# Re-ordered first stage, whole blocks at the first feed-forward's norm, two-part broadcasts, five pairs in token halves for six and three blocks for four

## The chip, the cores and the metric

The kernel runs on one core of one Trainium2 chip. The metric is the device time of one execution in microseconds (us), the median of several runs. One core has a matrix engine (PE, with its weight loads PEld), a vector engine (DVE), a scalar engine (ACT), a third elementwise engine (POOL), and a queue of transfers that is issued from SP. Each engine takes its own instructions strictly in the order in which the program put them.

## The reference

Two blocks follow each other on one sequence of T = 512 tokens with D = 1024 features, all in float32. Cut to what matters here:

```python
# first block
h = rmsnorm(x, norm1_g); z = h @ w_in + b_in
z_glu, z_rx, z_rg, z_ga, z_gb = split(z)
u   = z_glu[:, :D] * sigmoid(z_glu[:, D:])
u   = silu(layernorm(depthwise_conv31(u)))
y_a = u @ conv_w_out + conv_b_out
xb  = conv4(z_rx)                        # 1280 wide
hb  = rg_lru(xb, wa, wx, lambda)         # gates, then a scan over tokens
y_b = (hb * gelu(z_rg)) @ lru_w_out
x   = x + (sigmoid(z_ga) * y_a + sigmoid(z_gb) * y_b) @ w_mix_out
h   = rmsnorm(x, norm2_g)
x   = x + (silu(h @ ffn_w1) * (h @ ffn_w3)) @ ffn_w2
x   = rmsnorm(x, norm_f_g)
# second block; mods = silu(c) @ w_ada + b_ada gives nine vectors sh, sc, gt
h = rmsnorm(x, g_pre) * (1 + sc1) + sh1
x = x + 0.5 * gt1 * rmsnorm(swiglu(h, w_gu1, w_dn1), g_post)
h = rmsnorm(x, g_pre) * (1 + sc2) + sh2
x = x + gt2 * rmsnorm(token_mixer(h), g_post)    # linear attention + forgetting attention
h = rmsnorm(x, g_pre) * (1 + sc3) + sh3
x = x + 0.5 * gt3 * rmsnorm(swiglu(h, w_gu2, w_dn2), g_post)
```

## The kernel before

Features lie on the 128 partitions and tokens in the free dimension, so a 1024-wide activation is eight tiles of 128x512. Every product is made in three passes of a reduced float format (`mm3`, lines 128 to 130): high part of the weight with high part of the activation, the same weight with the low part, then the weight's low part with the high part. So each activation that feeds a product is kept as a pair (`hi`,`lo`; `u2h`,`u2l`; `m1h`,`m1l`; `pfh`,`pfl`; `hbh`,`hbl`), and each 128x1024 piece of weight that a transfer brings (`st`) is split into `whi` by ACT (line 123) and `wlo` by DVE (line 124; in the first stage POOL makes some). One block of eight feature tiles for 512 tokens is 24 matmuls of 128x512; a block in token halves is 24 of 128x256, twice.

The program is a list `steps`. `add(units, fn, own)` appends a step with the weights it wants. While the steps are emitted in that order, a background list `bg` is worked off between them by a credit that each step's matmuls give (`runbg`), `later` appends to it, `NEXT` in it ends the work of one step, and `flush` empties it. `defer(n, fn)` emits `fn` n steps later. Products write to three rotating accumulation buffers `mm`, everything else to five `ax`.

The first stage follows a string of step names. `g`m makes one eighth of the gated convolution input (two blocks, `ga` and `th`) and starts its 31 taps on DVE in `bg` (line 393). `r`j and `a`/`b` make the inputs and the gates of the recurrence, `s` the scans for five tiles in one step (line 547), `q`j the ten gelu blocks (`ge`, line 557), each multiplied with its scanned tile `xb` and split into `hbh`/`hbl` in the same step. Then eight times `yb_step` (blocks `w_in` 44+m and `lru_w_out`), eight `ga_step` blocks, and eight `ya_step` blocks (`conv_w_out`). The layer norm over the convolution's output (`ln_mean`, `ln_var`, `ln_rstd`, `ln_out`) is pushed to `bg` at the first `yb_step`. A norm's statistics are matmuls with one column per 128 tokens (`rstat`, line 187). The rows are turned into a full tile by a diagonal matrix made on DVE (`diag`, line 208) and one float32 matmul with ones (`bcast2`, line 214), which the trace records as two passes.

At each norm between products a `boundary` runs the last blocks of the product, and the first blocks behind the norm, in two token halves, so that the norm of one half lies beside matmuls of the other. `w_mix_out` runs all eight blocks so; `ffn_w2`, `w_dn1` and `w_dn2` run `NF` = 4 whole and four in halves; behind each norm `NH` = 6 pairs of feed-forward blocks (`ffn_pair`, lines 795 on) run in halves. An `ada_step` brings 512 KB of `w_ada` and multiplies it with `crow` on DVE (line 314); the 72 of them are laid between other steps, 1.75 per block in the first feed-forward.

Of the kernel before, what the change touches and what calls it, by code (L numbers as in the profile page):

```python
# [53 lines left out]
def build(tc, I, O, dbg=None):  # L54
# [128 lines left out]
    def rstat(pc, accs, r):  # L183
        nt = (r[1] - r[0]) // P
        for i, acc in enumerate(accs):
            for j in range(nt):
                mm(pc[:, i * nt + j:i * nt + j + 1], acc[:, r[0] + P * j:r[0] + P * (j + 1)], ones1,  # L187
                   start=True, stop=True)
# [196 lines left out]
    def delay(acc, u, d, w, b, first=False):  # L385
# [166 lines left out]
    def rg_step(j):  # L552
        def fn(W):
# [27 lines left out]
    def yb_step(m):  # L581
# [37 lines left out]
    def ln_out(m):  # L619
        V.tensor_tensor(CV[m], CV[m], H["lnr"], ALU.mult)  # L620
        s = act(CV[m], CV[m], AF.Silu, bias=col("conv_ln_b", m), scale=col("conv_ln_g", m))
        if m == 0:
            with tc.issue_after(s.ins):
                act(crow, crow, AF.Silu)
# [1015 lines left out]
```

## Time and profile before

| | |
|---|---|
| median of 3 runs | 2264.69 us (2263.28 to 2266.47) |
| the profiled execution | 2265.5 us |
| its span (first to last instruction) | 2263.8 us |
| mean granted clock of TensorE, share of full | 0.993 |
| PE busy | 2216.3 us, 98% |
| DVE busy | 1398.2 us, 62% |
| ACT busy | 943.5 us, 42% |
| POOL busy | 154.8 us, 7% |

Busy shares are means over stages with different limits. A matmul's recorded duration overlaps the next one's, so what a matmul costs is read from the distance of two starts. In a timeline row the bracket is the idle time of the engine just before it, with the instruction that ended it. The granted clock has two levels, 1.2 and 2.4 GHz; it is given as a share of the higher.

### The profile page before, as it was taken

To read this page: it belongs to the slowest core of one execution; us is meant where nothing else is said; L and a number is where in the kernel's file an instruction comes from. 1 tells how busy PE (TensorE), PEld (TensorE's weight loads), DVE (VectorE), ACT (ScalarE), POOL (GpSimd) and SP (SyncE) were. 2 spreads that over 40 slices of the span, in tenths; PEclk is the share of its full clock that TensorE was granted. 3 is DMA by queue.
4 is the path that set the end of the run, shared out by engine and by line. 5 is a ranking of instruction groups with operands and counts; after the bars stand their busy time and mean duration, and the time that the engine had idled before them with its cause. 6 is when DMAs were issued, how large, how long until landed. Compare 5 with 4: busy or idle time off the path is not lost.

```text
span 2263.8 us, 31021 instructions
## 1 busy us (share of the span) xinstructions
PE 2216.3 (98%) x12170; PEld 1915.6 (85%) x12170; DVE 1398.2 (62%) x2409; ACT 943.5 (42%) x1538; POOL 154.8 (7%) x178
## 2 busy tenths in 40 slices
PE   8899999999999999999999999999999999999997
PEld 6688788899887899988889987888888899988887
DVE  7999984866766448433326768675656558433234
ACT  6566423634322234332224567663434444323232
POOL 3243220000000000000100021100000000000000
PEclk9999999999999999999999999999999999999999
DMA  5343233524877534323233521213121322432342
GB/s 187 112 118 107 81 108 103 178 93 156 300 246 241 166 109 149 131 93 99 89 103 120 172 86 57 73 42 105 66 80 66 130 89 90 140 102 91 96 118 66
DMA packets 82451, 269.28 MB, mean 119 GB/s; under 512 B 10320, under 2 KB 12624, under 8 KB 82304
## 3 DMA queue, kind: packets, MB, share of 16 engines
q1 hardware_dynamic: 80896, 266.31, 36.6%
q8 instruction: 96, 1.57, 0.3%
q0 software_dynamic: 1264, 0.69, 0.1%
q10 hardware_dynamic: 144, 0.29, 0.1%
q14 instruction: 51, 0.42, 0.1%
HBM read 258.80 MB, written 4.19 MB: 116 GB/s over the span
## 4 chain that ended last, share of the span: by engine, by line
PE 86%; DVE 5%; DMA 2%; issue 1%; ACT 1%; DVEq 0%; ACTq 0%; SPq 0%
PE mm L128 26%; PE mm L129 26%; PE mm L130 26%; DMA st<-w_ada 2%; PE ax L1153 1%; PE ax L1155 1%; DVE wlo L124 1%; PE ax L1154 1%; PE ax L1208 1%; PE ax L214 1%; PE ax L1337 1%; PE ax L187 1%; DVE st L314 0%; DVE ax L393 0%; ACT p L1321 0%
## 5 line engine op out<-in xcount | busy, mean ns | idle before, releaser
L123 ACT ACTIVATE whi<-st 128x1024 fp32r<-128x1024 f32 (+4 forms) x424 | 431.1, 1018 | 838.2 <-PE mm L129 532.5
L124 DVE TENSOR_TENSOR wlo<-st,whi 128x1024 fp32r<-128x1024 f32 (+3 forms) x382 | 454.0, 1189 | 405.1 <-ACT whi L123 403.9
L128 PE MATMUL mm<-pfh,whi 128*128 128x512 f32 (+1 forms) x1676 | 568.9, 339 | 0.5 <-ACT sq L241 0.5
L129 PE MATMUL mm<-pfl,whi 128*128 128x512 f32 (+1 forms) x1676 | 565.6, 338 | 0.0
L130 PE MATMUL mm<-pfh,wlo 128*128 128x512 f32 (+1 forms) x1676 | 564.3, 337 | 1.2 <-DVE wlo L124 1.2
L130 PEld LDWEIGHTS mm<-pfh,wlo 128*128 128x128 f32 x1676 | 316.8, 189 | 34.3 <-DVE wlo L124 1.9
L128 PEld LDWEIGHTS mm<-pfh,whi 128*128 128x128 f32 x1676 | 317.2, 189 | 33.2 <-ACT sq L241 1.3
L129 PEld LDWEIGHTS mm<-pfl,whi 128*128 128x128 f32 x1676 | 317.2, 189 | 31.6 <-issue 0.5
L128 PE MATMUL mm<-m1h,whi 128*128 128x256 f32 (+1 forms) x528 | 177.2, 336 | 4.2 <-DVE fs L795 4.2
L128 PE MATMUL mm<-hi,whi 128*128 128x512 f32 x416 | 165.8, 398 | 15.4 <-ACT hi L341 6.4
L128 PE MATMUL mm<-mh,whi 128*128 128x256 f32 (+1 forms) x528 | 177.5, 337 | 2.0 <-ACT mh L765 1.1
L130 PE MATMUL mm<-mh,wlo 128*128 128x256 f32 (+1 forms) x528 | 177.3, 337 | 0.0
L129 PE MATMUL mm<-ml,whi 128*128 128x256 f32 (+1 forms) x528 | 177.1, 336 | 0.0
L129 PE MATMUL mm<-m1l,whi 128*128 128x256 f32 (+1 forms) x528 | 177.0, 335 | 0.0
L130 PE MATMUL mm<-m1h,wlo 128*128 128x256 f32 (+1 forms) x528 | 176.6, 334 | 0.0
L129 PE MATMUL mm<-lo,whi 128*128 128x512 f32 x416 | 165.9, 399 | 1.1 <-DVE lo L342 1.1
L130 PE MATMUL mm<-hi,wlo 128*128 128x512 f32 x416 | 165.5, 398 | 0.4 <-DVE wlo L124 0.4
L393 DVE SCALAR_TENSOR_TENSOR ax<-th,d_hdw,ax 128x500 f32<-128x500 f32 (+25 forms) x232 | 157.5, 731 | 1.1 <-ACT ax L391 0.2
L314 DVE SCALAR_TENSOR_TENSOR st<-st,crow 128x1024 f32<-128x1024 f32 x72 | 88.0, 1224 | 66.5 <-DMA st<-w_ada 66.0
L795 DVE TENSOR_TENSOR fs<-fs,mm 128x512 f32<-128x512 f32 (+1 forms) x84 | 47.9, 571 | 122.4 <-PE mm L130 122.3
L128 PEld LDWEIGHTS mm<-m1h,whi 128*128 128x128 f32 x528 | 100.2, 190 | 15.8 <-DVE fs L795 5.9
L128 PEld LDWEIGHTS mm<-mh,whi 128*128 128x128 f32 x528 | 100.8, 191 | 13.0 <-ACT mh L765 1.5
(359 smaller groups left out, 3432.8 us busy)
## 6 DMA issues: line engine op xcount, KB each, us to landing
st<-w_gu SPq DMA_DIRECT2D x102, 512.0 KB, 3.3
st<-w_ada SPq DMA_DIRECT2D x72, 512.0 KB, 4.5
st<-ffn_w SPq DMA_DIRECT2D x63, 512.0 KB, 4.1
st<-w_in SPq DMA_DIRECT2D x51, 512.0 KB, 3.3
st<-w2fm SPq DMA_DIRECT2D x51, 512.0 KB, 3.3
st<-w_dn SPq DMA_DIRECT2D x38, 448.0 KB, 3.3
st<-w_dn SPq DMA_DIRECT2D x24, 512.0 KB, 3.5
st<-w2v SPq DMA_DIRECT2D x16, 512.0 KB, 3.3
```

The costliest lines, as they stand in the source:

```text
L123: h = act(hi, src, AF.Copy)
L124: (eng or V).tensor_tensor(lo, src, hi, ALU.subtract)
L128: mm(out, whi, xh, start=start, stop=False)
L129: mm(out, whi, xl, start=False, stop=False)
L130: mm(out, wlo, xh, start=False, stop=stop)
L187: mm(pc[:, i * nt + j:i * nt + j + 1], acc[:, r[0] + P * j:r[0] + P * (j + 1)], ones1, start=True, stop=True)
L214: mm(R[:, :nt * P], ones, dg.rearrange("p n t -> p (n t)"), start=True, stop=True)
L314: V.scalar_tensor_tensor(w, w, 1.0, crow, ALU.mult, ALU.mult, accum_out=mods[:, n:n + 1])
L393: V.scalar_tensor_tensor(acc[:, d:], u[:, :T - d], w, acc[:, d:], ALU.mult, ALU.add)
L795: V.tensor_tensor(s, s, rs(st["u"], r), ALU.mult)
L1153: mm(o, h[:, sl], hi[c], start=k == 0, stop=False)
L1154: mm(o, l[:, sl], hi[c], start=False, stop=False)
```

## The change

Six things are edited.

- **First stage.** `g2` comes two steps earlier and the later `g` steps one; the first convolution taps go through `bg`; the scan of each of the five tiles is deferred by one to five steps; the `hbh`/`hbl` split of a gelu block is deferred by two steps. A zero fill moves from DVE to ACT.
- **`w_ada` steps.** Four lie beside `yb_step`, one behind each `ga_step`, six instead of eight beside `ya_step`, four beside `w_mix_out`, and 1.0 instead of 1.75 per block in the first feed-forward.
- **Broadcasts.** `diag` splits the row into a high and a low part (a cast and a subtraction, four wide) and makes two diagonals; `bcast2` multiplies both in the reduced format into one accumulator, in two single passes.
- **`behind_block`.** The matmuls of `rstat` and `bcast2` are placed behind the end of the product block that was last emitted.
- **First feed-forward's norm.** `w_mix_out` and the blocks behind it run whole. Three pairs multiply x times `norm2_g`, not yet normalized, and scale the result with the norm's rows (`ffn_raw`); the normalized tiles are made in `bg` meanwhile.
- **Halves.** `NH` goes from 6 to 5 and `NF` from 4 to 5.

```diff
+    zero = cp.tile([P, 1], F32, name="zero")
+    ones_r = cp.tile([P, P], F32R, name="ones_r")
...
+    block = [None]
     def mm3(out, whi, wlo, xh, xl, start, stop):
...
-        mm(out, wlo, xh, start=False, stop=stop)
+        block[0] = mm(out, wlo, xh, start=False, stop=stop)
+    def behind_block():
+        return tc.issue_after(block[0].ins) if block[0] is not None else nullcontext()
...
     def diag(y, nt):
-        dg = at(n="dg").rearrange("p (n t) -> p n t", t=P)[:, :nt]
-        V.tensor_tensor(dg, ident.unsqueeze(1).to_broadcast([P, nt, P]),
-                        y.unsqueeze(2).to_broadcast([P, nt, P]), ALU.mult)
-        return dg
+        yp = sp.tile([P, 2, 4], F32R, tag="yp", bufs=8, name=nm("yp"))
+        V.tensor_copy(yp[:, 0, :nt], y)
+        V.tensor_tensor(yp[:, 1, :nt], y, yp[:, 0, :nt], ALU.subtract)
...
+        for q in range(2):
+            dg = at(F32R, "dg").rearrange("p (n t) -> p n t", t=P)[:, :nt]
+            V.tensor_tensor(dg, ident.unsqueeze(1).to_broadcast([P, nt, P]),
+                            yp[:, q, :nt].unsqueeze(2).to_broadcast([P, nt, P]), ALU.mult)
     def bcast2(dg, nt):
         R = pax()
-        mm(R[:, :nt * P], ones, dg.rearrange("p n t -> p (n t)"), start=True, stop=True)
+        with behind_block():
+            for q in range(2):
+                mm(R[:, :nt * P], ones_r, dg[q], start=q == 0, stop=q == 1)
...
-            V.memset(acc[:, 0:d], 0.0)
+            act(acc[:, 0:d], zero[:, 0:d], AF.Copy)
...
             for m in range(5):
                 j = g * 5 + m
-                V.tensor_tensor(XB[j], XB[j], GT[2, j], ALU.mult)
-                V.tensor_tensor_scan(XB[j], GT[0, j], XB[j], 0.0, ALU.mult, ALU.add)
+                defer(1 + m, lambda j=j: scan(j))
...
-            HB[j] = (at(F32R, "hbh"), at(F32R, "hbl"))
-            split(ge, *HB[j])
+            def parts():
+                HB[j] = (at(F32R, "hbh"), at(F32R, "hbl"))
+                split(ge, *HB[j])
+            defer(2, parts)
...
-    for it in ("g0 r0 r1 r2 r3 r4 g1 a0 r5 a1 g2 a2 r6 a3 g3 a4 r7 r8 s0 g4 r9 b0 g5 b1 g6 b2 g7 b3 b4 "
+    for it in ("g0 r0 r1 r2 r3 r4 g1 g2 a0 r5 a1 g3 a2 r6 a3 g4 a4 r7 r8 s0 g5 r9 b0 g6 b1 b2 g7 b3 b4 "
...
-        if m >= 8:
+        if m % 2:
             ada_step()
...
     def ln_push(W):
+        bg.extend([NEXT, NEXT])
         later(0.9, ln_mean)
...
         add(wunits("w_in", 36 + m, KT, [8]), fn)
+        ada_step()
...
+    def ffn_raw(u, PF, j):
+        def fg(W):
+            gemm(pg, W, H["xg"])
+            V.tensor_tensor(s, pg, H["R"], ALU.mult)
+            act(s, s, AF.Silu)
+        def fu(W):
+            gemm(pu, W, H["xg"])
+            V.tensor_tensor(t, pu, H["R"], ALU.mult)
+            V.tensor_tensor(t, t, st["s"], ALU.mult)
+            split(t, *PF[j])
+        ada_step()
...
-    NH = 6
-    NF = 4
+    NH = 5
+    NF = 5
...
-    boundary("w_mix_out", M1, [8], mix_done, 0, n2_half, ffn_first(u1, PF1))
+    NR = 3
+    mix_steps()
+    add([], n2_rows)
+    for j in range(NR):
+        ffn_raw(u1, PF1, j)
...
-        H["ada"] = H.get("ada", 0.0) + 1.75
+        H["ada"] = H.get("ada", 0.0) + 1.0
...
-    ffn_rest(u1, PF1, ada_between)
+    for j in range(NR, NFF):
+        ffn_pair(u1, PF1, j, FULL, between=ada_between)
```

How the program's order moves is seen at three places. The first is PE at the layer norm of the convolution (`lnm` is the sum for its mean, `lnv` that for its variance, `hi`/`lo` are read by `ga_step`, `u2h`/`u2l` by `ya_step`). Before:

```order
L130 MATMUL mm_3060<-hi_433,wlo_2923 128x512
L187 MATMUL ax_3088<-ones,lnm_1582 128x1 x4
L128 MATMUL mm_3116<-hi_419,whi_2964 128x512
L129 MATMUL mm_3116<-lo_420,whi_2964 128x512
L130 MATMUL mm_3116<-hi_419,wlo_2965 128x512
L128 MATMUL mm_3116<-hi_421,whi_2964 128x512
L129 MATMUL mm_3116<-lo_422,whi_2964 128x512
L130 MATMUL mm_3116<-hi_421,wlo_2965 128x512
L128 MATMUL mm_3116<-hi_423,whi_2964 128x512
L214 MATMUL ax_3097<-dg_3095,ones 128x512
L129 MATMUL mm_3116<-lo_424,whi_2964 128x512
```

After:

```order
L136 MATMUL mm_3262<-hi_443,wlo_3174 128x512
L198 MATMUL ax_3289<-ones,lnm_1603 128x1 x4
L239 MATMUL ax_3303<-dg_3299,ones_r 128x512
L239 MATMUL ax_3303<-dg_3301,ones_r 128x512
L198 MATMUL ax_3340<-ones,lnv_3306 128x1 x4
L239 MATMUL ax_3367<-dg_3363,ones_r 128x512
L239 MATMUL ax_3367<-dg_3365,ones_r 128x512
L134 MATMUL mm_3424<-u2h_3372,whi_3213 128x512
L134 MATMUL mm_3466<-u2h_3372,whi_3256 128x512
L134 MATMUL mm_3508<-u2h_3372,whi_3418 128x512
L135 MATMUL mm_3424<-u2l_3373,whi_3213 128x512
```

The norm's four groups stood among the `ga_step` blocks; now they stand behind the last of these (`mm_3262`) with no product between them, and the first `ya_step` blocks follow.

The second is ACT at the first gelu blocks (`tt` belongs to the scans of the first five tiles). Before:

```order
L557 ACTIVATE ge_1843<-mm_1818,pcol 128x512
L123 ACTIVATE hbh_1846<-ge_1843 128x512
L123 ACTIVATE whi_1914<-st_1747 128x1024
L557 ACTIVATE ge_1885<-mm_1860,pcol 128x512
L543 ACT_TABLE_LOAD
L543 ACTIVATE tt_1399<-tt_1399 128x512
L123 ACTIVATE hbh_1888<-ge_1885 128x512
```

After:

```order
L595 ACTIVATE ge_1810<-mm_1785,pcol 128x512
L127 ACTIVATE whi_1860<-st_1721 128x1024
L595 ACTIVATE ge_1848<-mm_1823,pcol 128x512
L579 ACT_TABLE_LOAD
L579 ACTIVATE tt_1461<-tt_1461 128x512
L579 ACTIVATE tt_1596<-tt_1596 128x512
L579 ACTIVATE tt_1629<-tt_1629 128x512
L579 ACTIVATE tt_1741<-tt_1741 128x512
L579 ACTIVATE tt_1772<-tt_1772 128x512
L127 ACTIVATE hbh_1866<-ge_1810 128x512
```

The split `hbh` of a gelu block, which needs DVE's product with the scanned tile, stood right behind that block's gelu; now at least one more gelu goes ahead of it.

The third is PE at the boundary behind `w_dn1`, where the normalized first half of `h` is first read by the block of 48 columns. Before:

```order
L129 MATMUL mm_10389<-pfl_7928,whi_10535 128x256
L130 MATMUL mm_10389<-pfh_7927,wlo_10536 128x256
L128 MATMUL mm_10389<-pfh_7992,whi_10535 128x256
L214 MATMUL ax_10533<-dg_10504,ones 128x256
L129 MATMUL mm_10389<-pfl_7993,whi_10535 128x256
L130 MATMUL mm_10389<-pfh_7992,wlo_10536 128x256
```

After:

```order
L136 MATMUL mm_9655<-pfh_7845,wlo_9725 128x256
L239 MATMUL ax_9801<-dg_9772,ones_r 128x256 x2
L134 MATMUL mm_9944<-pfh_7017,whi_9774 48x256
L134 MATMUL mm_10005<-pfh_7017,whi_9804 128x256
L135 MATMUL mm_9944<-pfl_7018,whi_9774 48x256
L136 MATMUL mm_9944<-pfh_7017,wlo_9775 48x256
```

The broadcast was followed by 77 matmuls of the product's other half before the first 48-column one; now that one is next.

Counted over the whole order, product matmuls of 256 columns fall by 1548 and those of 512 rise by 774; broadcasts fall from 7 of 512 and 16 of 256 columns to 8 and 14.

## Rows read from the trace of the kernel before

**Rows 1.** Page, part 1: busy time, share and instructions of each engine.
```profile
PE 2216.3 (98%) x12170; PEld 1915.6 (85%) x12170; DVE 1398.2 (62%) x2409; ACT 943.5 (42%) x1538; POOL 154.8 (7%) x178
```

**Rows 2.** Timeline of PE (start, duration, instruction): six matmuls of a whole block apart.
```profile
999.91 0.39 PE L128 MATMUL mm<-pfh,whi 128*128 128x512 f32 x1
...
1001.27 0.39 PE L128 MATMUL mm<-pfh,whi 128*128 128x512 f32 x1
```

**Rows 3.** Timeline of PE: twelve matmuls of a block in halves apart.
```profile
869.87 0.28 PE L128 MATMUL mm<-pfh,whi 128*128 128x256 f32 x1
...
871.31 0.28 PE L128 MATMUL mm<-pfh,whi 128*128 128x256 f32 x1
```

**Rows 4.** Windows: length, busy PE PEld DVE ACT POOL (instructions), clock, DMA share, GB/s.
```profile
60.00:94.00 34.00, 24.47 (x86) 17.98 (x85) 33.84 (x51) 18.02 (x28) 7.87 (x7) 0.85 0.43 117
...
230.00:246.00 16.00, 12.26 (x43) 9.53 (x42) 16.00 (x20) 5.51 (x8) 3.67 (x2) 0.79 0.24 74
340.00:380.00 40.00, 40.00 (x180) 32.88 (x180) 14.23 (x16) 13.36 (x17) 4.16 (x3) 1.00 0.32 109
600.00:700.00 100.00, 99.30 (x437) 81.56 (x435) 65.62 (x96) 25.74 (x33) 0.00 (x0) 1.00 0.76 249
```

**Rows 5.** Timeline of PE at the first gelu blocks; the second row is 14 matmuls later.
```profile
236.49 0.79 PE L128 MATMUL mm<-hi,whi 128*128 128x512 f32 x1 [3.74 <-ACT ge L557]
...
242.56 0.40 PE L130 MATMUL mm<-hi,wlo 128*128 128x512 f32 x1
```

**Rows 6.** Timeline of PE at the layer norm, to the first `ya_step` block.
```profile
375.42 0.95 PE L187 MATMUL ax<-ones,lnm 128*128 128x1 f32 x8
376.23 0.49 PE L128 MATMUL mm<-hi,whi 128*128 128x512 f32 x1
...
377.71 0.39 PE L128 MATMUL mm<-hi,whi 128*128 128x512 f32 x1
377.95 1.02 PE L214 MATMUL ax<-dg,ones 128*128 128x512 f32 x2
...
379.03 0.40 PE L130 MATMUL mm<-hi,wlo 128*128 128x512 f32 x1
...
406.80 0.39 PE L128 MATMUL mm<-u2h,whi 128*128 128x512 f32 x1
```

**Rows 7.** Timeline of DVE at the end of the layer norm.
```profile
394.44 0.16 DVE L193 SCALAR_TENSOR_TENSOR s<-s,s 128x4 f32<-128x4 f32 x1
394.64 0.69 DVE L208 TENSOR_TENSOR dg<-ident,s 128x512 f32<-128x512 f32 x1
395.83 1.23 DVE L124 TENSOR_TENSOR wlo<-st,whi 128x1024 fp32r<-128x1024 f32 x1 [0.50 <-ACT whi L123]
396.98 4.27 DVE L620 TENSOR_TENSOR cv<-cv,ax 128x512 f32<-128x512 f32 x7
```

**Rows 8.** Timeline of PE: a half-width broadcast; one matmul lies between the rows.
```profile
505.60 0.67 PE L214 MATMUL ax<-dg,ones 128*128 128x256 f32 x2
...
506.23 0.28 PE L130 MATMUL mm<-m1h,wlo 128*128 128x256 f32 x1
```

**Rows 9.** Waits of PE: us in total, times, longest.
```profile
PE mm L128 <- DVE fs L795: 4.8, 5, 1.9
```

**Rows 10.** Timeline of DVE in the first feed-forward.
```profile
720.92 1.23 DVE L314 SCALAR_TENSOR_TENSOR st<-st,crow 128x1024 f32<-128x1024 f32 x1 [2.10 <-DMA st<-w_ada]
```

**Rows 11.** Timeline of PE behind `w_dn1`, then behind `w_out`.
```profile
1236.64 0.70 PE L214 MATMUL ax<-dg,ones 128*128 128x256 f32 x2 [0.23 <-DVE dg L208]
...
1247.13 0.28 PE L128 MATMUL mm<-pfh,whi 128*48 128x256 f32 x1
...
1873.92 0.67 PE L214 MATMUL ax<-dg,ones 128*128 128x256 f32 x2 [0.84 <-DVE dg L208]
1875.71 0.38 PE L128 MATMUL mm<-mh,whi 128*128 128x256 f32 x1 [1.12 <-ACT mh L765]
```

**Rows 12.** Timeline of DVE behind `w_dn1`: the last low parts of the first half.
```profile
1243.97 1.27 DVE L766 SCALAR_TENSOR_TENSOR pfl<-ht,mods,pfh 128x256 fp32r<-128x256 f32 x3
```

More of the change, by code (lines that the diff above doesn't have):

```diff
@@ L102, in build @@
     G.memset(ones, 1.0)
+    zero = cp.tile([P, 1], F32, name="zero")
+    G.memset(zero, 0.0)
+    ones_r = cp.tile([P, P], F32R, name="ones_r")
+    G.memset(ones_r.bitcast(F32), 1.0)
     eps1 = cp.tile([P, 1], F32, name="eps1")
@@ L184, in rstat @@
         nt = (r[1] - r[0]) // P
[L185 to L188, printed above, removed]
+        with behind_block():
+            for i, acc in enumerate(accs):
+                for j in range(nt):
+                    mm(pc[:, i * nt + j:i * nt + j + 1], acc[:, r[0] + P * j:r[0] + P * (j + 1)], ones1,
+                       start=True, stop=True)
     def newton(y, t, a):
@@ L313, in fn @@
             w = W[0][:, 0]
+            if n == 0:
+                with tc.issue_after(EV[0].ins):
+                    act(crow, crow, AF.Silu)
             V.scalar_tensor_tensor(w, w, 1.0, crow, ALU.mult, ALU.mult, accum_out=mods[:, n:n + 1])
@@ L436, in convolve, with first @@
             def convolve():
-                taps(0, 2)()
-                with behind(raw):
-                    taps(2, 4)()
+                if len(bg) > 3:
+                    bg.insert(len(bg) - 3, (0.0, taps(0, 2)))
+                else:
+                    taps(0, 2)()
+                    bg.append(NEXT)
+                def first():
+                    with behind(raw):
+                        taps(2, 4)()
+                later(1.44, first)
                 for d in range(4, 31, 4):
@@ L620, in ln_out @@
         V.tensor_tensor(CV[m], CV[m], H["lnr"], ALU.mult)
[L621 to L624, printed above, removed]
+        act(CV[m], CV[m], AF.Silu, bias=col("conv_ln_b", m), scale=col("conv_ln_g", m))
         U2.append((at(F32R, "u2h"), at(F32R, "u2l")))
@@ L662, in fn @@
             M1.append((hi, lo))
-        add(wunits("conv_w_out", m, KT, [8]), fn, own=1.8)
-        ada_step()
+        add(wunits("conv_w_out", m, KT, [8]), fn, own=2.1)
+        if m < 6:
+            ada_step()
     pool_steps[1] = len(steps)
@@ L735, in acc_sumsq, with mix_g, mix_steps, done @@
         sumsq(H[key], src, r, first, scale=scale)
-    def mix_done(ps, m, r):
-        V.tensor_tensor(rs(X[m], r), rs(X[m], r), ps, ALU.add)
-        acc_sumsq("acc", rs(X[m], r), m, r)
+    def mix_g(m):
+        h, l = H["xg"][m]
+        act(h, X[m], AF.Copy, scale=col("norm2_g", m))
+        V.scalar_tensor_tensor(l, X[m], col("norm2_g", m), h, ALU.mult, ALU.subtract)
+    def mix_steps():
+        def done(ps, m, r):
+            if m == 0:
+                H["xg"] = pairs(KT)
+            V.tensor_tensor(X[m], X[m], ps, ALU.add)
+            mix_g(m)
+            acc_sumsq("acc", X[m], m, FULL)
+        for m in range(KT):
+            product("w_mix_out", M1, [8], done, [m], FULL, 2.9)
+            if 1 < m < 6:
+                ada_step()
+    def n2_rows(W):
+        R = rms_rows(H["acc"], FULL)
+        H["R"] = at(n="R")
+        act(H["R"], R, AF.Copy)
+        del H["acc"]
+    def n2_tiles(m0):
+        def f():
+            if m0 == 0:
+                H["h"] = M1
+            for m in range(m0, m0 + 2):
+                t = at(n="ht")
+                V.scalar_tensor_tensor(t, X[m], col("norm2_g", m), H["R"], ALU.mult, ALU.mult)
+                post_split(m, t, FULL)
+        return f
+    def n2_end(W):
+        flush()
+        del H["xg"], H["R"]
+        SH[0] = lambda m: mods[:, m:m + 1]
+    def ffn_raw(u, PF, j):
+        st = {}
+        ug, uu = u(j)
+        def fg(W):
+            pg = pmm()
+            gemm(pg, W, H["xg"])
+            s = st["s"] = at(n="fs")
+            V.tensor_tensor(s, pg, H["R"], ALU.mult)
+            act(s, s, AF.Silu)
+        def fu(W):
+            pu = pmm()
+            gemm(pu, W, H["xg"])
+            t = at(n="fu")
+            V.tensor_tensor(t, pu, H["R"], ALU.mult)
+            V.tensor_tensor(t, t, st["s"], ALU.mult)
+            PF.append((at(F32R, "pfh"), at(F32R, "pfl")))
+            split(t, *PF[j])
+        add([ug], fg, own=0.7)
+        add([uu], fu, own=2.1)
+        ada_step()
     def normed(r, R, pre):
```

28 lines of the change are left out of this document (15 added, 13 removed).

## Prediction
> **What bounds the kernel now.** I read the page's busy times first: PE is busy for 98% of the span [rows 1], so the time is PE's, and a change can only give back time in which PE idles, runs at the low clock, or does the same product in a dearer form. I then read PE's timeline for what one matmul costs, by the distance of starts. In a whole block six matmuls take 1001.27 - 999.91 = 1.36 us, 0.2267 us each [rows 2]. In halves twelve take 1.44 us, 0.120 each [rows 3], so two halves cost 0.240, that is 13.3 ns more than one whole. Windows come next, for stretches where PE is not fed: in 60 to 94 us PE started 86 matmuls, worth 86 x 0.2267 = 19.5 us of 34, so 14.5 us were lost to waits and to a granted clock whose mean is 0.85; DVE is busy 33.84 of these 34 us. At the first gelu blocks it is the same picture, DVE busy 16.00 of 16 [rows 4]. Elsewhere in the front DVE has room: in 340 to 380 us it is busy 14.23 of 40 [rows 4]. Last I read the layer norm and the boundaries, since the order moves work there.
>
> **The change part by part.** All sums are against the profiled execution, 2265.5 us; the median of the runs is 0.8 lower.
>
> *Halves.* 774 pairs of half matmuls become whole ones: 774 x 13.3 ns = 10.3 us less, all of it on PE [rows 2, 3]. These blocks lie where PE is otherwise fed, so I count it fully.
>
> By the Trainium skill, "TensorE: Matmul & The Clock Gate", section "Back-to-back issue gap", an isolated matmul's gap is its columns over 2.4 GHz plus about 2.5 ns; a pair would then lose 2.5 ns, and 774 pairs 1.9 us, not 10.3. The rows here say 13.3 ns, so the trace does not agree, and the rows decide.
>
> *Broadcasts behind the layer norm.* A 512-wide one costs 379.03 - 377.71 less two matmuls of 0.2267 = 0.87 us [rows 6]; a 256-wide one 506.23 - 505.60 less 0.12 = 0.51, with any wait in it [rows 8]. Before there are 4 and 16 behind the layer norm: 3.5 + 8.2 = 11.7 us. The new form has two single passes. No row of before shows it; if a pass costs what a product matmul costs, 5 and 14 of them are 5 x 0.453 + 14 x 0.24 = 5.6 us, 6 less. Against it DVE makes two four-wide operations of 0.2 us (394.44 to 394.64) and a second diagonal before PE may start [rows 7], which costs where PE already waits for the diagonal, as behind `w_out` [rows 11]. Bounds are -6 and 0; I take -4.3, nearer the passes, since most broadcasts have product matmuls ahead of them.
>
> *Fewer `w_ada` steps in the first feed-forward.* PE waits 4.8 us there for `fs` on DVE [rows 9], and DVE stands before it in front of a `w_ada` tile that has not landed, 2.10 us in the row [rows 10]; traffic is 249 GB/s [rows 4]. A block of 24 matmuls takes 5.44 us and brings 0.5 MB of its own, and 0.875 MB of `w_ada` before, 0.5 after: some 258 GB/s become 193. I take -4.4 of the 4.8; bounds -4.8 and 0.
>
> *`w_dn1` boundary.* Before, the first 48-column block starts 10.5 us after the broadcast that its input needs [rows 11]; the 77 half matmuls between cover the chain. In the new order that block is next. From broadcast to first product took 1.8 us behind `w_out`, where nothing covers it either [rows 11], and the last low part of this half came 1243.97 + 1.27 - 1236.64 = 8.6 us after the broadcast [rows 12], while the first 48 interleaved half matmuls need 5.8. So 1.8 to 2.8 for the tail, plus a later broadcast by the longer diagonal, plus low clock: +4, bounds 0 and +8.
>
> *Un-normalized first blocks, handover, tail.* `w_mix_out` whole puts the end of the last tile, the statistics and the broadcast beside the first pair, which needs only x times a column. What is late next is the eviction of that pair, which waits for the norm's rows, and the eight normalized tiles before the fourth pair. I cost both at +1, bounds -1 and +4; the cover is about 130 us of matmuls, and DVE has a third of its time free in 600 to 700 us [rows 4].
>
> *Front, until the last `ga_step` block.* Its parts are three. The wait at the gelu blocks is 3.74 us, then 14 matmuls take 6.07 us instead of 3.17 at the low clock [rows 5]: 6.6 us. ACT there held a `hbh` split, which waits for DVE behind five scans, in front of the next gelu. With the split two blocks later and the scans spread, I count all 6.6 as gone. The layer norm's two statistics (376.23 - 375.42 = 0.8 each) and two broadcasts (0.87 each) no longer cut into these blocks [rows 6]: 3.3. For the 14.5 us of 60 to 94 the bounds are 0 and all of it: `g2` two steps earlier gives PE two more blocks (10.9 us) to do before `a0`, but DVE is full, and each tap, gate and split still has to be done before its reader. Following the new order through ACT and DVE with the rows' durations I find three waits left there, about 7 us, so -8 rather than -14.5. The last `ga_step` block then ends at 406.8 - 17.9 = 388.9.
>
> *Layer norm.* This is the price. Before, its chain lay beside `ga_step` blocks, and `ya_step` began at 406.80 without a wait [rows 6]. In the new order PE has only the norm's own matmuls between the last `ga_step` and the first `ya_step`, so it idles for the chain. From the first statistics to the first `cv` times the norm's factor took 396.98 - 375.42 = 21.6 us [rows 6, 7]. In it DVE did four weight splits of 1.15 (395.83 to 396.98), now one: -3.4. Two row splits of 0.4 and two more diagonals of 0.6: +2.0. Two single-pass broadcasts: -0.8. Then one `cv` pass of 0.6 and two ACT passes of about that length before the first matmul: +1.9. Sum 21.3, bounds 18 and 25. Behind so long an idle time I expect the low clock: rows 5 price it at 2.9 after a shorter one, and with `u2` tiles arriving one by one I take +3.4, bounds 2.9 and 7. DVE also gets 12 `w_ada` steps of 1.15 us before the norm (13.8 us), and six weight splits (6.9) that stood behind the norm's start. I cost them at nothing, since 25.8 us are free in 340 to 380 [rows 4]; without that cover they delay the norm one for one. `ya_step` starts at 388.9 + 21.3 = 410.2.
>
> *Sum.* Front -8 - 6.6 - 3.3 + 21.3 + 3.4 = +6.8. Behind it -10.3 - 4.3 - 4.4 + 4 + 1 = -14.0. Together -7.2: 2258.3 for a profiled execution, 2257.5 as median.
>
> **The rivals.** *A, the front is freed:* the 60 to 94 us waits go nearly whole and the `w_dn1` chain is covered after all: -6.5 and -3, 2248. For it: two more blocks of cover are worth 10.9 us. Against: DVE is full there [rows 4].
>
> *B, slower:* DVE reaches the end of the convolution's taps late. The norm needs the last tap's sum, PE has nothing else to do, and each us is paid in full. DVE is full until the scans, gets 20.7 us more to do, and PE arrives some 18 us earlier. Against it stand the idle 25.8 us. It decides once `ya_step` starts 12 us later than I say, past 422; at 12 to 20 late the time is 2270 to 2278.
>
> *C, the waits in 60 to 94 only move:* 0 of the 8, 2265.5, no change. For it: DVE's full window. Against: the earlier `g2` is product work that needs little of DVE.
>
> *D, halves cost next to nothing:* the 13.3 ns would belong to those stretches (weights or operands there), not to the width, and whole blocks in the same places would keep most of it; at 2.5 ns a pair the sum loses 8.4: 2266. That is what the skill's gap rule, cited above, would make of it. Against: the two spacings are steady where nothing waits [rows 2, 3].
>
> **How the numbers follow.** Forecast 0.45 (2251 to 2263 by itself), A 0.20, B 0.17, C 0.12, D 0.06. A measurement of this kernel can tell about 0.2% from no change, 4.5 us: faster is below 2260.2, slower above 2269.2. Faster: A and three quarters of the forecast, 0.54. Slower: B, 0.17. Within: the rest, 0.29. For the range I reach down into A and up to B's lower edge, 2244 to 2271; it leaves out A's lower part and most of B.
>
> **What would show it.** In the profile after: one idle stretch of PE of about 20 us at the layer norm, ended by ACT's `u2h`, with a low clock behind it, and `ya_step` near 410; no wait for `ge`; whole blocks still 0.2267 us a matmul; PE's waits for `fs` near zero; a wait of some us right behind `w_dn1`'s first broadcast. The prediction is wrong if PE does something else in that stretch, if the norm starts clearly after the last `ga_step` block, or if 60 to 94 us still loses 14.

## The result, and the profile after

The change made the kernel slower: 2282.13 us median (2280.86 to 2285.66) beside 2264.12 for the kernel before, a ratio of 1.0088 (95% interval 1.0074 to 1.0101). I had forecast 2257.5 within 2244 to 2271. The span of the profiled execution went from 2263.8 to 2279.2 us, 15.4 more.

The page of the kernel after shows that PE did not get more to do. Its busy time fell by 9.1 us against [rows 1]; its idle time rose.

```profile
PE 2207.2 (97%) x11394; PEld 1878.8 (82%) x11394; DVE 1396.3 (61%) x2379; ACT 928.4 (41%) x1494; POOL 159.6 (7%) x180
```

The starts of the same blocks in PE's two timelines tell where the 15.4 us arise:

| PE's first matmul of | before | after | ahead or behind |
|---|---|---|---|
| the gelu blocks | 199.95 | 199.61 | -0.3 |
| `ga_step` | 359.10 | 356.13 | -3.0 |
| `ya_step` | 406.80 | 423.47 | +16.7 |
| `w_mix_out` | 450.46 | 468.54 | +18.1 |
| `ffn_w2` | 747.78 | 753.89 | +6.1 |
| a block late in the attention (`pfh`) | 1592.95 | 1609.78 | +16.8 |
| end of the span | 2263.8 | 2279.2 | +15.4 |

There are two losses, 19.7 us between the start of `ga_step` and that of `ya_step`, and 10.7 between `ffn_w2` and the attention, and one gain, 12.0 us from `w_mix_out` to `ffn_w2`.

The first loss is the bare layer norm. PE's timeline from the last `ga_step` block on (start, duration, instruction, and in brackets idle time and what ended it; only rows with a wait):

```profile
400.42 1.05 PE L198 MATMUL ax<-ones,lnm 128*128 128x1 f32 x8 [0.60 <-POOL lnm L494]
402.73 1.40 PE L239 MATMUL ax<-dg,ones_r 128*128 128x512 f32 x2 [1.26 <-DVE dg L230]
413.94 1.84 PE L198 MATMUL ax<-ones,lnv 128*128 128x1 f32 x8 [9.82 <-DVE lnv L267]
419.31 1.30 PE L239 MATMUL ax<-dg,ones_r 128*128 128x512 f32 x2 [3.53 <-DVE dg L230]
423.47 1.65 PE L134 MATMUL mm<-u2h,whi 128*128 128x512 f32 x3 [2.85 <-ACT u2h L127]
```

The same four groups lay among product matmuls before [rows 6]. From the first statistics to the first `ya_step` matmul it is 23.05 us, and DVE's timeline shows why: the norm is a chain on DVE, one pass behind the other, with nothing in PE's order that it could do meanwhile.

```profile
404.33 2.47 DVE L654 TENSOR_TENSOR cv<-cv,ax 128x512 f32<-128x512 f32 x4
...
411.52 2.28 DVE L267 TENSOR_TENSOR lnv<-lnv,sq 128x512 f32<-128x512 f32 x3
...
418.48 1.29 DVE L230 TENSOR_TENSOR dg<-ident,yp 128x512 fp32r<-128x512 f32 x2
420.65 3.08 DVE L661 TENSOR_TENSOR cv<-cv,ax 128x512 f32<-128x512 f32 x5 [0.89 <-PE ax L239]
```

What DVE did just ahead of the chain matters too. The sum for the mean (`lnm`) needs the last total of the convolution (`cv`, L462), and that stands on DVE behind ten `w_ada` steps that each waited for their tile to land: 22.0 us of such waits between 345 and 400 us, and none there in the kernel before.

```profile
395.96 1.23 DVE L342 SCALAR_TENSOR_TENSOR st<-st,crow 128x1024 f32<-128x1024 f32 x1 [2.50 <-DMA st<-w_ada]
...
398.25 0.68 DVE L462 TENSOR_TENSOR cv<-cv,ax 128x512 f32<-128x512 f32 x1
```

PE came only 0.60 us too early for `lnm` in this run. In the trace of "Four blocks in halves again", whose first stage is the same, PE came 2.8 us earlier than here and the norm began no sooner:

```profile
400.72 1.87 PE L198 MATMUL ax<-ones,lnm 128*128 128x1 f32 x8 [3.71 <-POOL lnm L494]
```

Windows of the kernel after (length; busy us and instructions of PE, PEld, DVE, ACT, POOL; clock; DMA share; GB/s) stand beside [rows 4]:

```profile
60.00:94.00 34.00, 26.55 (x101) 20.69 (x100) 32.45 (x47) 15.06 (x25) 8.09 (x7) 0.90 0.44 124
230.00:246.00 16.00, 16.00 (x72) 13.27 (x71) 15.82 (x19) 6.87 (x11) 4.46 (x2) 1.00 0.14 49
380.00:427.00 47.00, 28.94 (x117) 22.83 (x116) 31.94 (x61) 17.59 (x27) 1.29 (x1) 0.75 0.35 112
600.00:700.00 100.00, 100.00 (x443) 82.81 (x442) 56.45 (x75) 29.20 (x37) 0.00 (x0) 1.00 0.63 197
1200.00:1300.00 100.00, 90.64 (x708) 88.28 (x707) 66.70 (x171) 45.14 (x88) 1.04 (x2) 0.97 0.37 119
```

The wait at the first gelu blocks is gone (72 matmuls instead of 43 in 230 to 246). In the first feed-forward PE does not wait any more and the traffic is 197 GB/s instead of 249. Behind `w_dn1` PE is busy for 90.64 of 100 us. The kernel before, in its own window, was nearly full:

```profile
1200.00:1300.00 100.00, 98.47 (x806) 97.07 (x805) 70.08 (x170) 51.47 (x101) 0.99 (x2) 1.00 0.43 142
```

### The profile page after: what moved, and what is told of

It reads as the page before. It is cut to its first block, busy times and chain, and to the rows that moved or that the text cites. A ratio compares the mean times of both kernels' runs of the same rounds, so it can differ in the third digit from the quotient of the medians.

```text
span 2279.2 us, 29354 instructions
## 1 busy us (share of the span) xinstructions
PE 2207.2 (97%) x11394; PEld 1878.8 (82%) x11394; DVE 1396.3 (61%) x2379; ACT 928.4 (41%) x1494; POOL 159.6 (7%) x180
## 4 chain that ended last, share of the span: by engine, by line
PE 80%; DVE 11%; DMA 2%; issue 2%; ACT 1%; POOL 0%; DVEq 0%; ACTq 0%; POOLq 0%
PE mm L134 24%; PE mm L135 24%; PE mm L136 23%; DVE ax L421 3%; DMA st<-w_ada 2%; DVE wlo L128 1%; PE ax L1246 1%; PE ax L1247 1%; PE ax L1248 1%; PE ax L1301 1%; PE ax L1430 1%; PE ax L198 1%; DVE xb L582 1%; PE ax L239 0%; DVE xb L581 0%
## 5 line engine op out<-in xcount | busy, mean ns | idle before, releaser
L128 DVE TENSOR_TENSOR wlo<-st,whi 128x1024 fp32r<-128x1024 f32 (+4 forms) x365 | 434.2, 1191 | 414.6 <-ACT whi L127 413.8
L134 PE MATMUL mm<-pfh,whi 128*128 128x512 f32 (+2 forms) x1592 | 553.9, 348 | 5.6 <-DVE qb L1128 2.8
L135 PE MATMUL mm<-pfl,whi 128*128 128x512 f32 (+2 forms) x1592 | 552.1, 347 | 0.6 <-DVE pfl L868 0.6
L136 PE MATMUL mm<-pfh,wlo 128*128 128x512 f32 (+2 forms) x1592 | 551.5, 347 | 0.8 <-DVE wlo L128 0.8
L134 PEld LDWEIGHTS mm<-pfh,whi 128*128 128x128 f32 (+1 forms) x1592 | 302.5, 190 | 40.9 <-issue 3.0
L136 PEld LDWEIGHTS mm<-pfh,wlo 128*128 128x128 f32 (+1 forms) x1592 | 302.5, 190 | 36.8 <-DVE wlo L128 1.2
L135 PEld LDWEIGHTS mm<-pfl,whi 128*128 128x128 f32 (+1 forms) x1592 | 302.4, 190 | 35.1 <-DVE pfl L868 1.0
L134 PE MATMUL mm<-mh,whi 128*128 128x512 f32 (+1 forms) x512 | 174.6, 342 | 3.4 <-ACT fs L890 2.0
L136 PE MATMUL mm<-mh,wlo 128*128 128x512 f32 (+1 forms) x512 | 174.2, 341 | 0.0
L135 PE MATMUL mm<-ml,whi 128*128 128x512 f32 (+1 forms) x512 | 173.9, 341 | 0.0
L134 PEld LDWEIGHTS mm<-mh,whi 128*128 128x128 f32 x512 | 97.8, 191 | 14.6 <-ACT fs L890 2.2
```

The source lines that it names most:

```text
L128: (eng or V).tensor_tensor(lo, src, hi, ALU.subtract)
L136: block[0] = mm(out, wlo, xh, start=False, stop=stop)
```

## The experiments

Ratios are against the kernel before on the same chip. "PE's loss" in a stretch is the sum, over its matmuls, of the distance between two starts less what that form takes when nothing waits (0.2267 us for 512, 0.120 for 256 columns). It is 3.6 us for the kernel before and 14.6 for the one after in 1200 to 1300 us.

### The layer norm back among the `ga_step` blocks

```diff
-        bg.extend([NEXT, NEXT])          # ahead of the layer norm
...
-        if m % 2:                        # beside yb_step
-            ada_step()
-        ada_step()                       # behind ga_step
-        H["ada"] = H.get("ada", 0.0) + 1.0
+        H["ada"] = H.get("ada", 0.0) + 1.3
-        runbg((slack - prep) * (1.3 if ln_steps[0] <= i < ln_steps[1] else 1.0))
+        runbg((slack - prep) * (3.0 if ln_steps[0] <= i < ln_steps[1] else 1.0))
```

> Edit on the changed kernel: the twelve w_ada steps beside yb_step and ga_step go into the first feed-forward (1.3 per block instead of 1.0), the two NEXT entries ahead of the layer norm go, and the credit factor in that stage is 3.0 instead of 1.3; in the order the norm's statistics and broadcasts then stand among the ga_step blocks again. Theory (the norm's bare chain costs the time): PE's idle stretch of 23 us before the first ya_step block goes to under 3 us, ya_step starts near 405 us instead of 423.5, and the time falls by 14 to 20 us to 2262 to 2268; the first feed-forward may give 0 to 3 us back to w_ada waits. Rival (DVE is behind with the taps, so the norm cannot start earlier whatever its place): the wait moves to PE's statistics matmul among the ga_step blocks, ya_step still starts after 418, and the time falls by 5 us or less, 2277 or more.

Measured 2271.85 us, ratio 1.0045 (1.0028 to 1.0062). PE's timeline, rows with a wait:

```profile
390.21 0.95 PE L198 MATMUL ax<-ones,lnv 128*128 128x1 f32 x8
406.69 0.80 PE L134 MATMUL mm<-u2h,whi 128*128 128x512 f32 x1 [4.91 <-ACT tha L684]
```

The second statistics now run 16 us ahead of `ya_step`, which starts at 406.69 instead of 423.47. So DVE's taps were not behind. This run changes the norm's place and takes the twelve `w_ada` steps out of DVE's way at once; the last experiment parts the two. Which of the two edits, the `NEXT` entries or the `w_ada` steps, put the norm behind the last `ga_step` block was not tried singly. By the ratios the time fell by 10 to 14 us and not by the 17 at `ya_step`: the twelve `w_ada` steps that had to go into the first feed-forward brought its waits for `fs` back (3.5 us). My lower bound of 14 us was too high. The 4.91 us left before `ya_step` are not the chain alone: the first `u2h` is done by 402.9, but the wait ends with ACT's `tha`, which reads the accumulation buffer of an earlier `ga_step` block and stands on ACT behind the norm's next tiles:

```profile
405.97 0.67 ACT L684 ACTIVATE tha<-mm,d_hb_in 128x512 f32<-128x512 f32 x1
```

### Four blocks in halves again

```diff
-    NF = 5
+    NF = 4
```

> Edit on the changed kernel: NF 4 instead of 5, so four blocks of ffn_w2, w_dn1 and w_dn2 run in halves again. Theory (cover lost at w_dn1): the waits of 1.2, 2.2, 0.6, 1.7, 0.9 and 3.0 us between 1250 and 1297 us and the low clock behind them go mostly, minus 9, against 66 more pairs in each of three places, 3 x 66 x 13.3 ns = 2.6 us: 2275, range 2273 to 2278. Rival (those waits come from the placing behind a block, or from the longer diagonal, not from the number of blocks): they stay, and the time rises by 2.6 us to 2285.

Measured 2281.12 us, ratio 1.0084 (1.0065 to 1.0104), no clear difference to the changed kernel (1.0088, 1.0106). PE's loss in 1200 to 1300 us went from 14.6 to 12.4 only. The wait before the 48-column block went, but one of 2.9 us (for ACT's `sq`) took its place, and the 2.8 for DVE's `qb` stayed. Neither account had this: the cover came back, and the loss did not go.

### Only the old string of steps

```diff
-    "g0 r0 r1 r2 r3 r4 g1 g2 a0 r5 a1 g3 a2 r6 a3 g4 a4 r7 r8 s0 g5 r9 b0 g6 b1 b2 g7 b3 b4 "
+    "g0 r0 r1 r2 r3 r4 g1 a0 r5 a1 g2 a2 r6 a3 g3 a4 r7 r8 s0 g4 r9 b0 g5 b1 g6 b2 g7 b3 b4 "
```

> Edit on the changed kernel: only the string of the first stage's steps is that of before. Theory (with DVE full the waits of the first 200 us only move with the order): the first gelu block starts within 2 us of the 199.6 of both kernels, and the time is 2282 within 3 us. Rival (the order does save the 8 us that I had put on it, and something else in the new first stage takes it back): the first gelu block starts at 205 or later and the time is 2288 or more.

Measured 2283.01 us, ratio 1.0096 (1.0080 to 1.0112), between the two of the changed kernel. The first gelu block did start later, at 205.2 us, behind a wait of 4.18 us for `gt`, as the rival had it; by the first `ga_step` block the two were level (357.6 beside 357.8 in the changed kernel's second trace), and the time is the theory's. The order moves waits within the first stage and takes none out of it as a whole. (The string moves more than the list of the change says: `g2` and `g3` come three steps earlier, `g4` four, `g5` two, `g6` one, and `g7` stays.)

### Float32 broadcasts again

```diff
-        for q in range(2):               # diag: two diagonals of the split row
+        V.tensor_tensor(dg, ident..., y..., ALU.mult)
-                mm(R[:, :nt * P], ones_r, dg[q], start=q == 0, stop=q == 1)
+            mm(R[:, :nt * P], ones, dg, start=True, stop=True)
```

> Edit on the changed kernel: diag and bcast2 in float32 as before (one diagonal, one matmul in two passes), still placed behind the last block. My forecast (PE time of the passes decides): slower by 4 us, 2286. Rival (DVE's longer chain decides, since PE waits 16 us for dg in all after the change and 4.5 us before): faster by 3 to 8 us, 2274 to 2279, with PE's waits for dg down by about 0.6 to 1.0 us each.

Measured 2275.28 us (2272.22 to 2281.69), ratio 1.0064 (1.0041 to 1.0086). That is below the changed kernel's 1.0088 and 1.0106, against my forecast, but the intervals overlap; the runs spread widely here, and the profiled one was the slowest of them. In that trace the stretch from `ffn_w2` to the attention is 4.3 us shorter than in the changed kernel's first trace (851.6 beside 855.9).

### The changed kernel again

> The changed kernel itself, beside the others on the same chip, so that small differences can be read: 2279 to 2283.

Measured 2282.93 us, ratio 1.0106 (1.0083 to 1.0129); with the first run that gives 1.0088 to 1.0106 for the changed kernel, between chips. Its trace has the same waits as its first one.

### The whole first stage as before

All hunks of the diff up to the layer norm are undone, with 1.3 `w_ada` steps per block; broadcasts, placing, whole blocks and halves stay new.

> Edit on the changed kernel: the whole first stage as before (string, taps, scans, splits, zero fill, no w_ada step beside yb_step and ga_step, no NEXT ahead of the norm), with 1.3 w_ada steps per block in the first feed-forward; broadcasts, placing, whole blocks and halves stay new. Theory (the first stage's new order is worth nothing beside the norm, and the later loss sits behind w_dn1): ya_step starts near 407, and the time is that of e1_ln_early within 3 us. Rival (the new order of the first stage does help, and only the norm's place hurt): 5 us or more slower than e1_ln_early.

Measured 2273.54 us, ratio 1.0061 (1.0038 to 1.0084), `ya_step` at 408.43. By the ratios that is 0.16%, 3.6 us, above the first experiment, with overlapping intervals: beside the norm's place no gain of the first stage's new order can be told from noise.

### No placing behind the last block

```diff
     def behind_block():
-        return tc.issue_after(block[0].ins) if block[0] is not None else nullcontext()
+        return nullcontext()
```

> Edit on the changed kernel: behind_block places nothing, so statistics and broadcasts go where the scheduler puts them. Theory (their late place is part of the loss behind w_dn1: the statistics of the second half stand 26 rows earlier in the new order without it): PE's loss between 1200 and 1300 us falls from 14.6 to about 10, elsewhere little changes, 2276 to 2279 beside 2281. Rival (the placing costs nothing, the statistics matmuls cut into blocks instead): within 2 us of the changed kernel. The layer norm's idle stretch of 23 us stays in both.

Measured 2281.49 us, ratio 1.0094 (1.0075 to 1.0112); PE's loss in 1200 to 1300 us 15.3. The placing by itself is not a cause.

### The first feed-forward's part alone

The kernel before with `mix_steps`, `ffn_raw`, and the `w_ada` steps that go with them.

> The kernel before with one part of the change alone: w_mix_out and the first feed-forward whole, three pairs not normalized, and the w_ada steps that belong to it (six beside ya_step, four beside w_mix_out, 1.3 per block). Theory (this part carries the whole gain: 480 pairs x 13.3 ns = 6.4 us and most of 4.8 us of waits for fs, less about 2 for the handover): faster than before by 7 to 11 us, first product of ffn_w2 at 737 to 741 us instead of 747.8. Rival (the gain in that stretch came from the broadcasts or from having w_ada out of the way earlier): faster by 4 us or less.

Measured 2259.82 us, ratio 0.9994 (0.9983 to 1.0005): no difference that can be told, and short of the 7 us forecast. From `w_mix_out` to `ffn_w2` it took 291.2 us instead of 297.3, about the 6.4 us of 480 pairs; the waits for `fs` did not go. Of PE's waits (us in total, times, longest), beside [rows 9]:

```profile
PE mm L134 <- DVE fs L854: 4.9, 5, 1.9
```

In this trace the first stage was 2.7 us later at `ya_step` than in the kernel before, which I can't put down to an edit.

### Early norm, and the boundary as before

The first experiment's edits, with `NF` 4, float32 broadcasts and no placing.

> The changed kernel with the edits of e1_ln_early, and with NF 4, float32 broadcasts and no placing, so that the boundary behind w_dn1 stands as before; the new first stage, the first feed-forward and NH 5 stay. Theory (two causes, the norm's bare chain and the lost cover behind w_dn1, make up the whole loss): PE's loss between 1200 and 1300 us falls from 14.7 to under 5, ya_step starts near 407, and the time is that of the kernel before less 0 to 4 us: 2258 to 2264. Rival (a third cause, such as the new first stage or the w_ada traffic): still 2267 or more.

Measured 2259.48 us, ratio 0.9981 (0.9972 to 0.9990), 0.19% faster than the kernel before and the fastest version found. The window behind `w_dn1` is full again (PE's loss 3.7 us), so the two losses together make up the whole of the result (the run undoes several edits at once and does not part them):

```profile
1200.00:1300.00 100.00, 98.49 (x799) 96.70 (x799) 71.69 (x171) 52.32 (x104) 0.98 (x2) 1.00 0.45 145
```

### The broadcasts alone

The kernel before with the changed `diag` and `bcast2`, nothing else.

> The kernel before with the two-part broadcasts alone. My forecast's step (the passes on PE decide): faster by 4 us, by up to 6. What e4_fp32_bcast points to (DVE's longer chain ahead of the broadcast decides at every boundary): slower by 3 to 7 us, with PE's waits for dg up from 4.5 to about 12 us.

Measured 2271.95 us, ratio 1.0033 (1.0021 to 1.0045): slower by 7.5 us. PE's passes did get cheaper; these are the groups of the two widths (count, busy us, mean ns, idle before), first of the kernel before, then of this one:

```profile
L214 PE MATMUL ax<-dg,ones 128*128 128x256 f32 x32 | 10.8, 431 | 4.9 <-DVE dg L208 4.5
L214 PE MATMUL ax<-dg,ones 128*128 128x512 f32 x14 | 7.4, 612 | 0.2
```

```profile
L229 PE MATMUL ax<-dg,ones_r 128*128 128x256 f32 x32 | 7.9, 330 | 7.4 <-DVE dg L216 7.0
L229 PE MATMUL ax<-dg,ones_r 128*128 128x512 f32 x14 | 5.9, 432 | 0.6 <-DVE dg L221 0.5
```

That is 4.4 us less busy time and 2.9 more idle time in front of them; I had expected those waits for `dg` to grow to about 12 us. Most of the loss is not at the broadcasts at all: PE's loss in 1200 to 1300 us is 7.0 us above that of the kernel before. Its largest parts are two waits a little behind the broadcasts of `w_dn1`, on PE, with low clock behind the first (mean 0.91 in 1240 to 1260 us):

```profile
1240.78 0.39 PE L130 MATMUL mm<-pfh,whi 128*128 128x256 f32 x1 [2.94 <-ACT sq L256]
```

The other, of 2.8 us, stands at 1284.5 and ends with DVE's `qb`. In the kernel before the first one is 0.47 us. ACT's timelines show the difference. `sq<-mm` reads an accumulation buffer that the next block needs. Before, it stands behind two of the norm's high parts:

```profile
1237.89 0.91 ACT L765 ACTIVATE pfh<-ht,mods 128x256 fp32r<-128x256 f32 x2 [2.19 <-DVE ht L946]
1238.71 0.36 ACT L241 ACTIVATE sq<-mm 128x256 f32<-128x256 f32 x1
1238.97 0.90 ACT L765 ACTIVATE pfh<-ht,mods 128x256 fp32r<-128x256 f32 x2
```

With the two-part broadcasts a weight split and four high parts go ahead of it:

```profile
1237.81 1.06 ACT L125 ACTIVATE whi<-st 128x1024 fp32r<-128x1024 f32 x1 [2.45 <-issue]
1238.77 1.69 ACT L780 ACTIVATE pfh<-ht,mods 128x256 fp32r<-128x256 f32 x4
1240.37 0.36 ACT L256 ACTIVATE sq<-mm 128x256 f32<-128x256 f32 x1
```

This order on ACT is the program's own, and `diag` and `bcast2` are all that was edited, so it came of them; that it is the longer chain on DVE that led the scheduler to it is my reading. The wait for `qb` is of the same kind. DVE's timeline of this kernel has a weight split, itself waiting for ACT, ahead of the second `qb`:

```profile
1280.92 0.42 DVE L1050 SCALAR_TENSOR_TENSOR qb<-mm,qa 64x256 fp32r<-64x256 f32 x1
1282.66 1.22 DVE L126 TENSOR_TENSOR wlo<-st,whi 128x1024 fp32r<-128x1024 f32 x1 [1.32 <-ACT whi L125]
1283.92 0.43 DVE L1050 SCALAR_TENSOR_TENSOR qb<-mm,qa 64x256 fp32r<-64x256 f32 x1
```

In the kernel before the two `qb` follow each other:

```profile
1276.82 0.42 DVE L1035 SCALAR_TENSOR_TENSOR qb<-mm,qa 64x256 fp32r<-64x256 f32 x1
1277.68 0.43 DVE L1035 SCALAR_TENSOR_TENSOR qb<-mm,qa 64x256 fp32r<-64x256 f32 x1 [0.45 <-ACT qa L1034]
```

That the orders differ and that PE waits for just these instructions is shown; a kernel with the longer chain and the old order was not tried, so how much of the 7.5 us is the order's alone stays open.

### The `w_ada` steps spread

The first feed-forward's part alone, with eight `w_ada` steps beside `w_mix_out` instead of four, eight beside `ya_step` instead of six, two per raw pair instead of one, and 1.0 per block instead of 1.3.

> e7_ffn1_only with the w_ada steps laid elsewhere: eight beside ya_step, eight beside w_mix_out, two per pair not normalized, and so 1.0 instead of 1.3 per block in the rest of the first feed-forward. Theory (the waits for fs, 4 to 5 us in e7_ffn1_only, come from w_ada tiles that have not landed): these waits go to under 1 us, the stretch from the first w_mix_out block to the first ffn_w2 block shortens from 291 to 286 us, and the time is 5 to 8 us below the kernel before, 2254 to 2258. Rival (the waits go along with the steps): within 2 us of e7_ffn1_only.

Measured 2263.52 us, ratio 0.9998 (0.9989 to 1.0007). The waits for `fs` are gone, and the stretch is 291.6 us as before the spreading. PE and DVE show where most of the gain went; with the low clock behind this wait PE's loss in 450 to 500 us is 4.4 us instead of the 0.3 before the spreading:

```profile
459.79 0.79 PE L134 MATMUL mm<-m1h,whi 128*128 128x512 f32 x1 [2.64 <-ACT m1h L674]
```

```profile
457.24 1.22 DVE L329 SCALAR_TENSOR_TENSOR st<-st,crow 128x1024 f32<-128x1024 f32 x1
458.39 0.08 DVE L329 DVE_READ_ACCUMULATOR st<-st,crow 128x1 f32 x1
458.39 0.68 DVE L672 TENSOR_TENSOR ya<-ya,thb 128x512 f32<-128x512 f32 x1
```

A `w_ada` step now stands in front of the last `ya` tile, which PE needs. The steps carry their price with them, and the rival had it.

### Early norm, with the `w_ada` steps kept in the first stage

```diff
-        runbg((slack - prep) * (1.3 if ln_steps[0] <= i < ln_steps[1] else 1.0))
+        runbg((slack - prep) * (6.0 if ln_steps[0] <= i < ln_steps[1] else 1.0))
```

The line is that of the changed kernel; "Early norm, and the boundary as before" had 3.0 there. The rest is that kernel, with the `w_ada` steps where the change put them.

> As e8_early_and_cover, but with the w_ada steps where the change put them (beside yb_step and ga_step, 1.0 per block in the first feed-forward), and the credit factor 6.0 so that the norm still comes ahead of the last ga_step block: its second statistics stand 24 matmuls, 5.4 us, before the first ya_step matmul. Theory (the w_ada steps of the first stage cost nothing by themselves once the norm does not wait for them, and they free the first feed-forward): the waits for fs there, 4 us in e8_early_and_cover, are gone; of the norm's tail of about 8 us some 3 us show before ya_step; time within 3 us of e8_early_and_cover. Rival (the w_ada steps delay the norm's own work on DVE): ya_step starts at 415 or later and the time is 5 us or more above e8_early_and_cover.

Measured 2263.95 us, ratio 1.0010 (1.0001 to 1.0019); by the ratios that is 0.3%, 6.5 us, above that kernel. `ya_step` starts at 414.50 (408.95 there) behind a wait of 4.23 us, again for ACT's `tha`; the waits for `fs` are gone and the stretch from `w_mix_out` to `ffn_w2` is 285.9 us, beside 290.8. The norm's first statistics ran at 385.3 instead of 378.5. `ya_step` misses the rival's 415 by little, and the rest of the rival holds: the steps delay the norm, by 7 us, and give less back. DVE's waits for `w_ada` tiles are there again (16.0 us in 345 to 400, beside 5.8). So of the 17 us that `ya_step` was late in the changed kernel the norm's place has about 9 (423.47 to 414.50) and the `w_ada` steps most of the rest; the shares are rough, since these kernels differ in the broadcasts and the credit too.

## Why the prediction was wrong, step by step

**Layer norm: right.** Forecast 21.3 us of bare chain within 18 to 25; measured 23.05. The low clock behind it was priced at 3.4; the `ya_step` blocks took 45.1 us instead of 43.7, so 1.4. Together 24.5 beside 24.7.

**Front, up to the last `ga_step` block: wrong by 11.5 us.** I had it end at 388.9, and the norm began at 400.4. The statistics and broadcasts that no longer cut into these blocks gave 3.4 us as forecast (44.3 instead of 47.7 for them). The step that failed first is the 8 us for the waits in 60 to 94. The waits themselves came as I had them, three of them, 7.4 us together; but I took these 7 from a loss of 14.5 that has the low clock behind the waits in it. The loss fell to 34 - 101 x 0.2267 = 11.1 only: 3.7 us of low clock had been left out. PE's timeline of the kernel after has the three, and two more later on that had not been there:

```profile
67.20 0.50 PE L134 MATMUL mm<-hi,whi 128*128 128x512 f32 x1 [3.75 <-DVE rx L410]
...
81.50 0.50 PE L134 MATMUL mm<-xbh,whi 128*128 128x512 f32 x1 [1.50 <-ACT th L445]
...
85.35 0.80 PE L134 MATMUL mm<-xbh,whi 128*128 128x512 f32 x1 [2.19 <-ACT ga L436]
...
177.66 0.79 PE L134 MATMUL mm<-xbh,whi 128*128 128x512 f32 x1 [2.76 <-ACT ga L436]
...
268.22 0.50 PE L135 MATMUL mm<-hbl,whi 128*128 128x512 f32 x1 [2.26 <-DVE hbl L128]
```

The wait of 177.66, with its low clock, took the 3.4 us back before the first gelu block (PE's loss from 94 to 200 us rose from 1.6 to 5.2), so up to there this was rival C: the earlier product work only moved the waits. The second failure is the wait at the gelu blocks. It went, as forecast, but of its 6.6 us only 2.6 were left at the first `ga_step` block, since the low part of the deferred split (`hbl`, 268.22) became late, with a stretch of low clock behind it: 4.2 us lost in 260 to 275. I had asked what is late next for the first of these and not for the second.

A third step is hidden behind these two. I costed the twelve `w_ada` steps ahead of the norm at nothing, for their 1.15 us of work each, and not for the landing of their tiles that DVE waits for. With the convolution's last total behind these tiles the norm could not begin before about 400 us, as the 3.71 us wait for `lnm` in the run with four blocks in halves shows. So PE would have waited away a front as short as I had forecast, unless the tiles had landed sooner too, which no run shows.

**Halves: right.** 480 of the pairs lie in the first feed-forward (6.4 us) and its stretch shortened by 6.1 in the kernel that had only this. Behind the attention 114 pairs are worth 1.5 us, and that part shortened by 1.4. Rival D is out: `w_mix_out` shows both spacings in one place, twelve half matmuls in 1.44 us in the kernel before, then six whole ones in 1.36 in the kernel after.

```profile
480.00 0.28 PE L128 MATMUL mm<-m1h,whi 128*128 128x256 f32 x1
...
481.44 0.28 PE L128 MATMUL mm<-m1h,whi 128*128 128x256 f32 x1
```

```profile
479.67 0.39 PE L134 MATMUL mm<-m1h,whi 128*128 128x512 f32 x1
...
481.03 0.39 PE L134 MATMUL mm<-m1h,whi 128*128 128x512 f32 x1
```

**`w_ada`: right where I looked, wrong in the whole.** The 4.8 us of waits for `fs` went (forecast 4.4). But the spread steps cost elsewhere as much, which the last two experiments show; I had costed them at nothing by DVE's idle 25.8 us. (My traffic of 258 GB/s before was also mis-worked: the sizes that give 193 after give 265. The trace had 249 and then 197, and no term hangs on it.)

**Broadcasts: wrong in sign.** Forecast -4.3, with bounds -6 and 0; alone they cost 7.5. The passes did get cheaper, by 4.4 us of PE's busy time. The bound was wrong: I let DVE's extra work cost at most what the passes save, and only as waits for the diagonal (these grew by 2.9 us). That the edit could change the order on ACT and DVE behind the broadcast was not in the sum, and there PE lost most of the 7.5.

**`w_dn1`: direction right, size and cause wrong.** Forecast +4 within 0 to 8, by lost cover. PE's loss there rose by 11.0 us. The lost cover is part of it, but giving it back alone returned 2.2 us, and giving back the broadcasts alone returned 2.4. Giving back both, with no placing, returned all 11. Either one alone leaves the weight split ahead of the second `qb` on DVE, and with four blocks in halves alone the late `sq` on ACT came as well. With the cover whole and the broadcasts alone changed the loss already rose by 7.0 of these 11, so the lost cover was not the main part of it, as I had it.

**Sum.** From the row of milestones: -0.3 to the gelu blocks (forecast -8), -2.6 there (-6.6), then -3.4 and +24.5 as forecast, -12.0 in the first feed-forward, +10.7 from `ffn_w2` to the attention, where my terms come to about -1 (180 pairs -2.4, somewhat over half of the broadcasts' -4.3, `w_dn1` +4), and -1.4 behind. That is +15.5, which the table has as +15.4 by rounding. Two terms, the front by 11.5 and the boundary with its broadcasts by some 11 or 12, are the whole difference to the forecast of -7.2. Rival B had the sign, and its mark was met, with `ya_step` past 422 and the norm beginning just as the convolution's sum came. But DVE was not late with the taps, the last of which ends at 351.4; it stood in front of the `w_ada` tiles ahead of the sum. And B left out the boundary behind `w_dn1`, about half of the difference.

## What to carry to other kernels

When an order puts a norm's whole chain between two groups of products, price it in full, and treat what is to pay for it, waits that a busy engine causes, as worth nothing until you have named what comes late next. An operation that is cheaper on the bounding engine and longer on another is a change of order too: look at which instructions on the other engines free the accumulation buffers, and whether they still stand where they stood. Work that is moved out of a crowded stretch takes its price along: count what stands behind it on its engine while its data has not landed, and try it alone before counting the gain.

## What the runs showed of the hardware

During the bare chain the granted clock was low for nearly the whole of it: 0.56 as mean of 400 to 427 us, and 0.50, the lower level, from 410 to 423. The `u2` matmuls at 424.91 and 425.34 are 0.43 us apart; those at 426.80 and 427.03 are 0.23 apart, the higher level. I had expected the slower start to cost 3.4 us; it cost 1.4. A broadcast in two single passes took 330 ns of recorded time per pass at 256 columns and 432 at 512, beside 431 and 612 for the float32 passes.
